# Attention core in plain fp32 with head pairs on two column tiles, and VectorE's share of the depthwise convolution summed in a PSUM bank

## The chip, the cores and the metric

The kernel is one program for one core of a Trainium2 chip. The metric is the device time of one execution in microseconds; several executions are taken and their median is given. The profile is of one further execution.

The engines are named as in the profile: PE is TensorE (matrix products; PEld its weight loads), DVE VectorE, ACT ScalarE, POOL GpSimd, SP SyncE, which issues the transfers. [...]

## The reference

A first block of two layers works on 512 tokens of 1024 channels; then a second block (a recurrent token mixer and a layer of experts) follows, which the change doesn't touch. Each layer of the first block is a mixer, a cross attention to 256 memory tokens and a feed-forward net. The mixer is what the change is about:

```python
def mla_group(c_q, c_kv, k_r, cos, sin, q_norm_g, w_uq, kv_norm_g, w_ukv):
    q = (rms_norm(c_q, q_norm_g) @ w_uq).reshape(B, S, MLA_HEADS, QK_NOPE_DIM + QK_ROPE_DIM)   # 8 heads, 64 + 32
    q_nope, q_rope = q[..., :QK_NOPE_DIM], apply_rope(q[..., QK_NOPE_DIM:], ...)
    kv = (rms_norm(c_kv, kv_norm_g) @ w_ukv).reshape(B, S, MLA_HEADS, QK_NOPE_DIM + V_HEAD_DIM)
    k_nope, v = kv[..., :QK_NOPE_DIM], kv[..., QK_NOPE_DIM:]
    k_rope = apply_rope(k_r, cos, sin)
    for start in range(0, S, Q_BLOCK):                      # 4 blocks of 128 queries
        end = start + Q_BLOCK
        s = einsum(q_nope[:, start:end], k_nope[:, :end]) + einsum(q_rope[:, start:end], k_rope[:, :end])
        s = where(mask, s * scale, -inf)                    # causal in chunks of 64
        p = softmax(s)
        outs.append(einsum('bhqk,bkhd->bqhd', p, v[:, :end]))

def conformer_conv_group(u, dw_w, dw_b, norm_g, norm_b):    # 512 channels, 31 taps
    a, g = split(u, 2)
    h = a * sigmoid(g)
    h = causal depthwise convolution of h with dw_w, + dw_b
    return silu(layer_norm(h, norm_g, norm_b))

def hybrid_mixer(x, ...):
    proj = x @ w_in + b_in                                  # c_q 256, c_kv 256, k_r 32, u 1024 columns
    return concatenate([mla_group(c_q, c_kv, k_r, ...), conformer_conv_group(u, ...)]) @ w_o
```

## The kernel before

The program is written with named tile pools, and a scheduler sets the order on each engine from a simulated timeline; the code gives data flow, tile pools and program order. The order of the built program is therefore shown below where it matters.

Most products are made at nearly fp32 accuracy from fp32r operands: each operand is kept as a high part and the remainder, and `mm3` (L155 to L159) issues three matmuls. `weight` (L134) loads a block of weights into a tile `wr`, ScalarE copies the high part (L148), and VectorE or GpSimd subtracts (L152); every `pool_lo`-th block goes to GpSimd. `split_ps` (L126) does the same from a PSUM bank: ScalarE copies the high part (L128), VectorE subtracts it (L130). `rstd` (L179) puts a power -1/2 on GpSimd (L185). A `ring` hands out the eight PSUM banks `q0` to `q7` in turn; `cm` is a pool of two 128 x 512 tiles.

`mixer` (L438) runs per layer. `latent(c)` projects the tokens onto 256 (c_q) or 288 columns (c_kv and k_r), squares and sums on ScalarE (L467), scales on VectorE (L469) and transposes. `gated(i)` projects two channel blocks of 128 (a block lies on the partitions, the 512 tokens along the row), applies the sigmoid (L487) and multiplies (L488); `conv_start` (L658) writes tap 30 and the bias into `acc`. The four blocks are the convolution's channels 0 to 3. The order in the code is latent(0), gated(0), latent(1), the keys' rotary part (L498 to L504, copied to four key tiles), the queries, gated(2), the keys' and values' weights, the values.

The attention goes through the heads. Two heads' keys come from `keys` (every second head; L573 copies the upper 64 rows down), the transposed query from `query`. For each of four blocks of queries: scores (one `mm3` on at least 256 keys), the row's maximum on VectorE (L604), the exponential with its sum on ScalarE (L607), the reciprocal on VectorE (L609), the scaling on ScalarE (L610), transposes on TensorE (L163), `split_ps` of the transposed probabilities. Then the output of a head: `mm3` with 128 columns of values, of which the head's own 64 are kept, and a `split_ps` of 64 rows. The code of the convolution, `conv` (L660), stands behind the heads, and the scheduler brings it forward into the gaps. VectorE has channel 0 and three quarters of channel 2, one operation a tap, with the running sum `acc` in SBUF (L669). GpSimd has channels 1 and 3 and the last quarter of channel 2: a product into a `cm` tile, by ScalarE (L673) for taps 10 to 29 of channel 1, by GpSimd itself (L675) otherwise, and an addition (L676). Behind it come the normalization over the channels (L638 to L647) and the output projection (`out_proj`).

## Time and profile before

| | us |
|---|---|
| median of 3 runs | 2641.08 |
| lowest and highest | 2638.80, 2645.98 |
| profiled execution | 2640.32 |
| its span, first to last instruction | 2638.1 |

| engine | busy us | share of the span |
|---|---|---|
| PE | 2460.6 | 93% |
| DVE | 1412.5 | 54% |
| ACT | 915.9 | 35% |
| POOL | 745.8 | 28% |

The mean granted clock of TensorE is 0.958 of full speed. The share of busy time is a mean over stages with different limits: for a change in the mixer the rows of the mixer's own stretch are to be read, which is about 37 to 260 us in layer 0 and 866 to 1090 us in layer 1. [...]

### The profile page before, as it was taken

The page shows a single profiled execution, that of the slowest core. Times are in us where ns is not written, and L with a number is a line of the kernel's source. Part 1 is how long each engine was busy: PE and PEld are TensorE (multiplying, and loading weights), DVE is VectorE, ACT ScalarE, POOL GpSimd, SP SyncE. Part 2 cuts the span into 40 slices and gives each one's busy share as a digit, 9 for nine tenths or more (in the row PEclk, how much of TensorE's full clock was granted, in tenths as well). Part 3 has the DMA queues.
Part 4 walks back from the last instruction along what each step waited for, and adds up shares of the span by engine and source line. Part 5 has one row for each costly group of instructions (what it writes and reads, how often), then busy time and mean ns, then how long its engine had stood idle before and what let it go on. Part 6 is the DMA issues. An engine that isn't in the chain of part 4 may idle for free.

```text
span 2638.1 us, 33264 instructions
## 1 busy us (share of the span) xinstructions
PE 2460.6 (93%) x12892; PEld 1858.1 (70%) x12892; DVE 1412.5 (54%) x2235; ACT 915.9 (35%) x1659; POOL 745.8 (28%) x627
## 2 busy tenths in 40 slices
...
GB/s 152 75 15 64 168 80 80 152 165 139 160 160 139 76 49 41 72 152 89 73 105 104 80 65 96 81 41 96 17 33 53 188 215 409 409 409 409 409 409 262
DMA packets 207513, 395.16 MB, mean 150 GB/s; under 512 B 24080, under 2 KB 115352, under 8 KB 207356
## 3 DMA queue, kind: packets, MB, share of 16 engines
...
q8 instruction: 101, 1.65, 0.3%
q14 instruction: 56, 0.46, 0.1%
...
## 4 chain that ended last, share of the span: by engine, by line
PE 76%; DVE 16%; ACT 3%; issue 2%; DMA 1%; POOL 1%; SPq 0%; DVEq 0%; POOLq 0%; ACTq 0%
PE q L157 17%; PE q L158 16%; PE q L159 16%; PE q L1756 12%; DVE t L669 4%; PE q L163 4%; PE q L1793 2%; DVE wl L152 1%; PE q L1731 1%; PE q L1183 1%; PE q L1188 1%; PE q L1757 1%; DVE t L130 1%; DVE xt L281 1%; DVE s L1159 1%
## 5 line engine op out<-in xcount | busy, mean ns | idle before, releaser
L157 PE MATMUL q<-t,wh 128*128 128x512 f32 (+1 forms) x1320 | 493.3, 375 | 16.1 <-DVE t L130 6.1
L159 PE MATMUL q<-t,wl 128*128 128x512 f32 (+1 forms) x1320 | 490.8, 374 | 8.8 <-DVE wl L152 5.6
L158 PE MATMUL q<-t,wh 128*128 128x512 f32 (+1 forms) x1320 | 492.8, 374 | 2.0 <-DVE t L1484 1.1
L148 ACT ACTIVATE wh<-wr 128x1024 fp32r<-128x1024 f32 (+4 forms) x280 | 289.0, 1034 | 491.7 <-PE q L159 213.2
L152 DVE TENSOR_TENSOR wl<-wr,wh 128x1024 fp32r<-128x1024 f32 (+2 forms) x206 | 266.3, 1296 | 207.8 <-ACT wh L148 203.3
L157 PE MATMUL q<-wh,t 128*128 128x512 f32 (+4 forms) x964 | 364.7, 383 | 8.9 <-ACT wh L148 3.7
L158 PE MATMUL q<-wl,t 128*128 128x512 f32 (+4 forms) x964 | 364.5, 379 | 4.5 <-DVE wl L538 2.2
L159 PE MATMUL q<-wh,t 128*128 128x512 f32 (+4 forms) x964 | 360.8, 379 | 0.6 <-DVE t L130 0.4
L152 POOL TENSOR_TENSOR wl<-wr,wh 128x1024 fp32r<-128x1024 f32 (+3 forms) x74 | 186.7, 2525 | 597.4 <-ACT wh L148 539.1
L157 PEld LDWEIGHTS q<-t,wh 128*128 128x128 f32 x1320 | 251.3, 191 | 66.2 <-DVE t L130 7.2
L159 PEld LDWEIGHTS q<-t,wl 128*128 128x128 f32 x1320 | 251.7, 191 | 51.4 <-DVE wl L152 6.9
L158 PEld LDWEIGHTS q<-t,wh 128*128 128x128 f32 x1320 | 251.6, 191 | 44.2 <-DVE t L1484 1.4
L185 POOL TENSOR_TENSOR sm<-sm,mhalf 128x1 f32<-128x1 f32 (+3 forms) x75 | 73.6, 983 | 738.4 <-DVE sm L183 736.9
L157 PEld LDWEIGHTS q<-wh,t 128*128 128x128 f32 x964 | 184.5, 192 | 50.3 <-DVE xt L292 6.4
L158 PEld LDWEIGHTS q<-wl,t 128*128 128x128 f32 x964 | 184.8, 192 | 38.3 <-DVE wl L538 2.7
L159 PEld LDWEIGHTS q<-wh,t 128*128 128x128 f32 x964 | 184.3, 192 | 35.3 <-issue 0.9
L676 POOL TENSOR_TENSOR t<-t,cm 128x128 f32<-128x128 f32 (+10 forms) x180 | 196.3, 1091 | 26.0 <-ACT cm L673 19.1
L803 POOL TENSOR_TENSOR t<-cm,t 128x512 fp32r<-128x512 f32 x44 | 70.5, 1603 | 302.6 <-ACT t L802 302.6
L163 PE MATMUL q<-ident,s 128*128 128x128 f32 (+3 forms) x538 | 98.1, 292 | 54.5 <-DVE s L1694 13.2
L128 ACT ACTIVATE t<-q 128x512 fp32r<-128x512 f32 (+1 forms) x172 | 89.4, 543 | 144.4 <-PE q L163 100.5
L163 PEld LDWEIGHTS q<-ident,s 128*128 128x128 f32 (+3 forms) x538 | 65.5, 147 | 100.7 <-issue 26.9
L130 DVE TENSOR_TENSOR t<-q,t 128x512 fp32r<-128x512 f32 (+1 forms) x172 | 103.6, 620 | 56.2 <-ACT t L128 55.8
...
## 6 DMA issues: line engine op xcount, KB each, us to landing
...
```

The lines of the kernel that those rows point to most:

```text
L128: nc.scalar.activation(hi, ps, AF.Copy, scale=1.0 if scale is None else scale)
L130: nc.vector.tensor_tensor(out=lo, in0=ps, in1=hi.bitcast(F32), op=OP.subtract)
L148: nc.scalar.activation(hi, raw, AF.Copy)
L152: e.tensor_tensor(out=lo, in0=raw, in1=hi.bitcast(F32), op=OP.subtract)
L157: m(out, ah, bh, start=first, stop=False)
L158: m(out, ah, bl, start=False, stop=False)
L159: m(out, al, bh, start=False, stop=last)
L163: self.nc.tensor.transpose(out, in_, self.ident[:n, :n])
L185: nc.gpsimd.tensor_tensor(out=r, in0=v, in1=self.mhalf[:, :n], op=OP.pow)
L669: e.scalar_tensor_tensor(a, h, w, a, op0=OP.mult, op1=OP.add)
L676: e.tensor_tensor(out=a, in0=a, in1=m, op=OP.add)
L1756: mm(ps[lo_, :], x, raw[:, c0], start=first, stop=last)
```

## The change

The queries, the keys, the values and the transposed probabilities are kept once, in fp32, and multiplied in plain fp32. The scores are one matmul on the valid keys only. The outputs are made for two heads at a time: each head's 64 columns of values go to one of two column tiles of TensorE and to the lower or upper 64 partitions of one bank, and one `split_ps` of 128 rows serves both. What was a `split_ps` ahead of it becomes one copy: the keys' lower half on VectorE (L571 of the new file) and upper half on ScalarE (L572), the query and the values on ScalarE (L581, L549), the transposed probabilities on VectorE (L609). Two key tiles instead of four hold two heads each, and the rotary part goes into them by two copies (L506, L507) in place of a split and three copies.

In the convolution VectorE has channels 0 and 2 whole: a product with the bias added (L662), 30 operations whose running sum is read from and written to PSUM bank 7 (L666; the last one writes `acc`), and a copy of the first 30 columns (L667). GpSimd has channels 1 and 3; ScalarE makes the products of taps 8 to 29 of channel 1 and 14 to 29 of channel 3. `gated(2)` stands right behind `gated(0)`, ahead of `latent(1)`; `pool_lo` becomes 5 ahead of `latent(1)`; the rings are cut so that bank 7 stays free.

```diff
@@ -455,7 +455,7 @@
         ck = self.t8([2, 2, 512])
         def latent(c):
             c0, n = (0, 256) if c == 0 else (256, 288)
-            ring = self.ring(*range(4 * c, 4 * c + 4))
+            ring = self.ring(0, 1, 2, 3)
             ps = self.tok_cols(w_in, c0, n, xT, ring, tokens_first=c == 0)
             ss = self.sm([NT])
             for t in range(NT):
@@ -479,7 +479,7 @@
         acc = self.t8([4, 512], F32)
 
         def gated(i):
-            ring = self.ring(0, 1, 2, 3)
+            ring = self.ring(4, 5, 6, 3)
             pa_ = self.fm_pair(w_in, 544 + i * 128, xT, ring)
             pg = self.fm_pair(w_in, 1056 + i * 128, xT, ring)
             for j in range(2):
@@ -487,24 +487,27 @@
                 nc.scalar.activation(sg, pg[j], AF.Sigmoid, bias=cv[:, i + j, 35:36])
                 nc.vector.scalar_tensor_tensor(hs[:, i + j, :], pa_[j], cv[:, i + j, 34:35], sg,
                                                op0=OP.add, op1=OP.mult)
-                self.conv_start(hs, acc, cv, i + j)
+                if i + j in self.CONV_POOL:
+                    self.conv_start(hs, acc, cv, i + j)
 
         latent(0)
         gated(0)
+        gated(2)
+        self.pool_lo = 5
         latent(1)
         kr = krt.rearrange("p t (h d) -> p t h d", h=1)
         self.rope(kr[:, :, :, 64:80], kr[:, :, :, 80:96], 0, NT, 1)
 
-        ps = self.ring(4)()
+        ps = self.ring(6)()
         for t in range(NT):
             self.tr(ps[:100, t * 128:(t + 1) * 128], krt[:, t, :])
-        kts = [self.n4([2, 512], F32R) for _ in range(4)]
-        self.split_ps(ps[64:100, :], kts[0][64:100, 0, :], kts[0][64:100, 1, :])
-        for k in kts[1:]:
-            nc.vector.tensor_copy(k[64:100], kts[0][64:100])
-        ring = self.ring(4, 5, 6, 7)
+        kts = [self.n4([2, 512]) for _ in range(2)]
+        tail = ps[64:100, None, :].to_broadcast([36, 2, 512])
+        nc.scalar.activation(kts[0][64:100], tail, AF.Copy)
+        nc.vector.tensor_copy(kts[1][64:100], tail)
+        ring = self.ring(4, 5, 6)
         qt = [self.t8([2, 8, 100], F32) for _ in range(2)]
         for i in range(2):
             nc.scalar.activation(qt[i][:, :, :, 96:100],
@@ -521,11 +524,8 @@
                                      ps.rearrange("p (h d) -> p h d", h=4), AF.Copy, scale=QSCALE)
         for i in range(2):
             self.rope(qt[i][:, :, :, 64:80], qt[i][:, :, :, 80:96], 2 * i, 2, 8)
-        gated(2)
-        self.stage(f"win_c{l}")
-        self.pool_lo = 5
         self.stage(f"win_u{l}")
-        ring = self.ring(4, 5, 6, 7)
+        ring = self.ring(0, 1, 2, 3)
         w_ukv = A["mla_w_ukv"][l].rearrange("(k p) (h d) -> p k h d", p=128, h=8)
 
         def kv_weight(d0):
@@ -540,39 +540,36 @@
 
         wkh, wkl = kv_weight(0)
         wvh, wvl = kv_weight(64)
-        vh, vl = self.t8([NT, 512]), self.t8([NT, 512])
+        vt = self.t8([NT, 512], F32)
         for t in range(NT):
             ps = ring()
             s = slice(t * 128, (t + 1) * 128)
             for k in range(2):
                 self.mm3(ps, ck[:, 0, k, s], ck[:, 1, k, s], wvh[:, k, :], wvl[:, k, :], k == 0, k == 1)
-            self.split_ps(ps, vh[:, t, :], vl[:, t, :])
+            nc.scalar.activation(vt[:, t, :], ps, AF.Copy)
 
         self.stage(f"qv{l}")
         yT = FM(self, 8, 512)
-        sring, tring, cring = self.ring(0, 1), self.ring(2, 3, 4, 5), self.ring(6, 7)
-        ptas = [[self.s2([2, 256], F32R) for _ in range(2)] for _ in range(2)]
-        ptbs = [self.t8([2, 4, 256]) for _ in range(2)]
+        sring, tring, cring = self.ring(0, 1), self.ring(2, 3, 4), self.ring(5, 6)
+        mm = nc.tensor.matmul
+        ptas = [[self.s2([2, 256]) for _ in range(2)] for _ in range(2)]
+        ptbs = [self.t8([2, 4, 256], F32) for _ in range(2)]
         for i in range(2):
             for j in range(2):
-                nc.gpsimd.tensor_copy(ptas[i][j][:, 1, 0:128], self.zeros.to_broadcast([128, 128]))
-                nc.gpsimd.tensor_copy(ptbs[i][:, j, 3, 0:128], self.zeros.to_broadcast([128, 128]))
+                nc.gpsimd.memset(ptas[i][j][:, 1, 0:128], 0.0)
+                nc.gpsimd.memset(ptbs[i][:, j, 3, 0:128], 0.0)
+        def key(h):
+            return kts[h % 4 // 2][:, h % 2, :]
 
         def keys(h):
             ps = cring()
             for k in range(2):
                 s = slice(h * 64, h * 64 + 128)
                 self.mm3(ps, wkh[:, k, s], wkl[:, k, s], ck[:, 0, k, :], ck[:, 1, k, :], k == 0, k == 1)
-            for i in range(2):
-                kk = kts[(h + i) % 4]
-                if i == 0:
-                    src = ps[0:64, :]
-                else:
-                    tmp = self.s2([512])
-                    nc.scalar.activation(tmp[0:64, :], ps[64:128, :], AF.Copy)
-                    src = tmp[0:64, :]
-                self.split_ps(src, kk[0:64, 0, :], kk[0:64, 1, :])
+            nc.vector.tensor_copy(key(h)[0:64], ps[0:64, :])
+            nc.scalar.activation(key(h + 1)[0:64], ps[64:128, :], AF.Copy)
 
         qs = {}
 
@@ -580,9 +577,9 @@
             ps = tring()
             for t in range(NT):
                 self.tr(ps[:100, t * 128:(t + 1) * 128], qt[t // 2][:, t % 2, h, :])
-            qh, ql = self.s2([512], F32R), self.s2([512], F32R)
-            self.split_ps(ps[:100, :], qh[:100, :], ql[:100, :])
-            qs[h] = qh, ql
+            q = self.s2([512])
+            nc.scalar.activation(q[:100, :], ps[:100, :], AF.Copy)
+            qs[h] = q
 
         keys(0)
         query(0)
@@ -591,15 +588,13 @@
                 if h % 2 == 1:
                     keys(h + 1)
                 query(h + 1)
-            kh, kl = kts[h % 4][:, 0, :], kts[h % 4][:, 1, :]
-            qh, ql = qs.pop(h)
-            ptb = ptbs[h % 2]
-            halves = (ptas[h % 2], (ptb[:, 0], ptb[:, 1]))
+            kh, q = key(h), qs.pop(h)
+            pair = h // 2 % 2
+            pts = [(ptas[pair][i], ptbs[pair][:, i]) for i in range(2)]
             for t in range(NT):
-                n, nv = max(256, (t + 1) * 128), (t + 1) * 128
-                s = slice(t * 128, (t + 1) * 128)
+                nv = (t + 1) * 128
                 ps = sring()
-                self.mm3(ps[:, :n], qh[:100, s], ql[:100, s], kh[:100, :n], kl[:100, :n], True, True)
+                mm(ps[:, :nv], q[:100, t * 128:nv], kh[:100, :nv], start=True, stop=True)
                 nm = self.sm([1])
                 nc.vector.tensor_reduce(nm, ps[:, :nv], axis=AX.X, op=OP.max, negate=True)
                 p = self.s2([512])
@@ -611,18 +606,18 @@
                 pt = tring().rearrange("p (k t) -> p k t", k=4)
                 for k in range(t + 1):
                     self.tr(pt[:, k, :], p[:, k * 128:(k + 1) * 128])
-                dh, dl = halves[t // 2]
-                s = slice((t % 2) * 128, (t % 2) * 128 + 128)
-                self.split_ps(pt[:, :t + 1, :], dh[:, :t + 1, s], dl[:, :t + 1, s])
-            ps = cring()
-            hp = slice((h // 2) * 128, (h // 2) * 128 + 128)
-            for i in range(2):
-                dh, dl = halves[i]
-                s = slice(i * 256, (i + 1) * 256)
-                for k in range(2 * i + 2):
-                    self.mm3(ps[:, s], vh[:, k, hp], vl[:, k, hp], dh[:, k, :], dl[:, k, :], k == 0, k == 2 * i + 1)
-            hs_ = slice((h % 2) * 64, (h % 2) * 64 + 64)
-            self.split_ps(ps[hs_, :], yT.hi(h // 2)[hs_, :], yT.lo(h // 2)[hs_, :])
+                nc.vector.tensor_copy(pts[h % 2][t // 2][:, :t + 1, (t % 2) * 128:(t % 2) * 128 + 128], pt[:, :t + 1, :])
+            if h % 2:
+                ps = cring()
+                for i in range(2):
+                    n = 2 * i + 2
+                    for k in range(n):
+                        for j in range(2):
+                            hd = slice((h - 1 + j) * 64, (h + j) * 64)
+                            mm(ps[j * 64:j * 64 + 64, i * 256:(i + 1) * 256], vt[:, k, hd], pts[j][i][:, k, :],
+                               start=k == 0, stop=k == n - 1)
+                self.split_ps(ps, yT.hi(h // 2), yT.lo(h // 2))
         self.conv(hs, acc, cv)
 
         self.stage(f"attn{l}")
@@ -648,10 +643,9 @@
         return yT
 
 
-    CONV_DVE = (((0, 0, 512),), ((2, 0, 384),))
-    CONV_POOL = (((1, 0, 512),), ((3, 0, 512),), ((2, 384, 512),))
-    conv_act = [(1, j) for j in range(10, TAPS)]
+    CONV_DVE = (0, 2)
+    CONV_POOL = (1, 3)
+    conv_act = [(1, j) for j in range(8, TAPS)] + [(3, j) for j in range(14, TAPS)]
 
     def conv_start(self, hs, acc, cv, i):
 
@@ -659,27 +653,27 @@
 
     def conv(self, hs, acc, cv):
 
         nc = self.nc
-        def tap(e, i, t0, t1, j):
-            h, a, w, d = hs[:, i, :], acc[:, i, :], cv[:, i, j:j + 1], 30 - j
-            a0 = max(t0, d)
-            a, h = a[:, a0:t1], h[:, a0 - d:t1 - d]
-            if e is nc.vector:
-                e.scalar_tensor_tensor(a, h, w, a, op0=OP.mult, op1=OP.add)
-            else:
-                m = self.cm()[:, :t1 - a0]
+        ring = self.ring(7)
+        for i in self.CONV_DVE:
+            sums = ring()
+            w = lambda j: cv[:, i, j:j + 1]
+            nc.vector.tensor_scalar(sums, hs[:, i, :], w(30), w(31), op0=OP.mult, op1=OP.add)
+            for j in range(29, -1, -1):
+                d = 30 - j
+                out = sums[:, d:] if j else acc[:, i, d:]
+                nc.vector.scalar_tensor_tensor(out, hs[:, i, :512 - d], w(j), sums[:, d:], op0=OP.mult, op1=OP.add)
+            nc.vector.tensor_copy(acc[:, i, :30], sums[:, :30])
+        for i in self.CONV_POOL:
+            for j in range(29, -1, -1):
+                d = 30 - j
+                m = self.cm()[:, :512 - d]
                 if (i, j) in self.conv_act:
-                    nc.scalar.activation(m, h, AF.Copy, scale=w)
+                    nc.scalar.activation(m, hs[:, i, :512 - d], AF.Copy, scale=cv[:, i, j:j + 1])
                 else:
-                    e.tensor_scalar(m, h, w, 1.0, op0=OP.mult, op1=OP.mult)
-                e.tensor_tensor(out=a, in0=a, in1=m, op=OP.add)
-        for e, groups in ((nc.vector, self.CONV_DVE), (nc.gpsimd, self.CONV_POOL)):
-            for pieces in groups:
-                for j in range(29, -1, -1):
-                    for i, t0, t1 in pieces:
-                        tap(e, i, t0, t1, j)
+                    nc.gpsimd.tensor_scalar(m, hs[:, i, :512 - d], cv[:, i, j:j + 1], 1.0, op0=OP.mult, op1=OP.mult)
+                nc.gpsimd.tensor_tensor(out=acc[:, i, d:], in0=acc[:, i, d:], in1=m, op=OP.add)
 
     def memory_keys(self, l):
 
```

New line numbers of the attention: scores L597, maximum L599, exponential L602, reciprocal L604, scaling L605, copy of the probabilities L609, outputs L618.

VectorE, layer 0, about the first maximum of the attention (before L604, now L599); `t_202` is the gated input, `t_203` is `acc`. Before:

```order
L130 TENSOR_TENSOR s_1015<-q_1009,s_1014 100x512
L669 SCALAR_TENSOR_TENSOR t_203<-t_202,cvec,t_203 128x378
L130 TENSOR_TENSOR n_690<-s_1005,n_690 64x512
L130 TENSOR_TENSOR s_1024<-q_1018,s_1023 100x512
L669 SCALAR_TENSOR_TENSOR t_203<-t_202,cvec,t_203 128x377
L604 TENSOR_REDUCE sm<-q_1027 128x1
L130 TENSOR_TENSOR n_691<-q_1118,n_691 64x512
L669 SCALAR_TENSOR_TENSOR t_203<-t_202,cvec,t_203 128x376
L609 RECIPROCAL sm<-sm 128x1
L604 TENSOR_REDUCE sm<-q_1043 128x1
L669 SCALAR_TENSOR_TENSOR t_203<-t_202,cvec,t_203 128x375
```

Now, with `q_1633` for the sums of channel 2 in bank 7:

```order
L666 SCALAR_TENSOR_TENSOR q_1633<-t_202,cvec,q_1633 128x484
L666 SCALAR_TENSOR_TENSOR q_1633<-t_202,cvec,q_1633 128x483
L666 SCALAR_TENSOR_TENSOR t_203<-t_202,cvec,q_1633 128x482
L667 COPY t_203<-q_1633 128x30
L599 TENSOR_REDUCE sm<-q_1007 128x1
L604 RECIPROCAL sm<-sm 128x1
L599 TENSOR_REDUCE sm<-q_1020 128x1
L609 COPY s_970<-q_1017 128x128
L604 RECIPROCAL sm<-sm 128x1
L599 TENSOR_REDUCE sm<-q_1034 128x1
L571 COPY n_819<-q_1219 64x512
```

Before, part of the convolution stands between the operations of the first heads; now all 62 of its operations stand ahead of the first maximum, and the heads follow without it.

ScalarE, layer 0, about the first exponential (before L607, now L602). Before:

```order
L128 ACTIVATE s_1014<-q_1009 100x512
L128 ACTIVATE n_690<-s_1005 64x512
L128 ACTIVATE s_1023<-q_1018 100x512
L128 ACTIVATE n_691<-q_1118 64x512
L607 ACT_TABLE_LOAD
L607 ACTIVATE s_1033,sm<-q_1027,sm 128x128
L610 ACTIVATE s_1033<-s_1033,sm 128x128
L607 ACTIVATE s_1049,sm<-q_1043,sm 128x256
L128 ACTIVATE s_982<-q_1039 128x128
L610 ACTIVATE s_1049<-s_1049,sm 128x256
L607 ACTIVATE s_1066,sm<-q_1060,sm 128x384
```

Now, with `cm` for products that GpSimd adds:

```order
L673 ACTIVATE cm<-t_202,cvec 128x500
L581 ACTIVATE s_998<-q_993 100x512
L581 ACTIVATE s_1005<-q_1000 100x512
L673 ACTIVATE cm<-t_202,cvec 128x499
L602 ACT_TABLE_LOAD
L602 ACTIVATE s_1011,sm<-q_1007,sm 128x128
L673 ACTIVATE cm<-t_202,cvec 128x498
L605 ACTIVATE s_1011<-s_1011,sm 128x128
L602 ACTIVATE s_1024,sm<-q_1020,sm 128x256
L673 ACTIVATE cm<-t_202,cvec 128x497
L605 ACTIVATE s_1024<-s_1024,sm 128x256
```

Before, no product of the convolution is left here; now 13 of channel 3's 16 products stand ahead of the first exponential and three between the first operations of head 0.

## Rows read from the trace of the kernel before

**Rows 1.** The head of the page.
```profile
span 2638.1 us, 33264 instructions
```

**Rows 2.** Chain of waits, 20 to 260 us, shares of that stretch by line.
```profile
by line: DVE t L669 21.0%; PE q L157 10.0%; PE q L158 9.7%; PE q L159 9.3%; issue 7.4%; DVE wl L152 4.5%; PE q L163 3.4%; DVE t L130 3.2%; DVE n L130 2.8%; ACT s L607 2.7%; ACT s L610 2.6%; ACT t L128 2.0%; DVE s L130 1.7%; DVE s L469 1.7%;
```

**Rows 3.** Windows: us, busy us (records) of PE, PEld, DVE, ACT, POOL; clock.
```profile
120.00:140.00 20.00, 12.06 (x41) 8.75 (x40) 19.93 (x25) 8.50 (x14) 19.77 (x22) 0.77 0.37 111
140.00:160.00 20.00, 15.90 (x55) 12.48 (x55) 19.87 (x38) 11.10 (x27) 19.84 (x16) 0.50 0.00 0
```

**Rows 4.** Two longer windows of layer 0, columns as in rows 3.
```profile
58.60:143.50 84.90, 67.83 (x317) 56.27 (x315) 83.36 (x101) 43.37 (x73) 70.96 (x55) 0.88 0.27 75
183.00:231.00 48.00, 42.97 (x257) 35.76 (x258) 33.21 (x81) 37.54 (x94) 40.71 (x66) 0.96 0.18 56
```

**Rows 5.** Line L669 alone in windows: VectorE's busy us (operations), clock, DMA.
```profile
58.60:143.50 84.90, 44.37 (x37) 0.88 0.27 75
143.50:231.00 87.50, 20.43 (x24) 0.84 0.10 31
183.00:231.00 48.00, 0.00 (x0) 0.96 0.18 56
```

**Rows 6.** Timeline of VectorE: start, us, line, tiles, count.
```profile
66.05 0.74 DVE L488 SCALAR_TENSOR_TENSOR t<-q,cvec,s 128x512 f32<-128x512 f32 x1
...
923.71 6.11 DVE L669 SCALAR_TENSOR_TENSOR t<-t,cvec,t 128x490 f32<-128x490 f32 x3
...
930.07 2.23 DVE L669 SCALAR_TENSOR_TENSOR t<-t,cvec,t 128x487 f32<-128x487 f32 x3
```

**Rows 7.** VectorE by line and form, 58.6 to 143.5 us: count, busy us, mean ns.
```profile
L152 DVE TENSOR_TENSOR wl<-wr,wh 128x1024 fp32r<-128x1024 f32 x5 | 6.5, 1298 | 0.0
...
L504 DVE CAST n<-n 36x1024 fp32r<-36x1024 f32 x3 | 3.5, 1225 | 0.0
```

**Rows 8.** Timeline of VectorE: first maximum, head outputs; layer 0, then layer 1.
```profile
143.46 0.27 DVE L604 TENSOR_REDUCE sm<-q 128x1 f32<-128x128 f32 x1
...
182.74 0.67 DVE L130 TENSOR_TENSOR t<-q,t 64x512 fp32r<-64x512 f32 x1
...
231.03 0.69 DVE L130 TENSOR_TENSOR t<-q,t 64x512 fp32r<-64x512 f32 x1 [0.36 <-ACT t L128]
...
973.62 0.27 DVE L604 TENSOR_REDUCE sm<-q 128x1 f32<-128x128 f32 x1
...
1058.22 0.69 DVE L130 TENSOR_TENSOR t<-q,t 64x512 fp32r<-64x512 f32 x1
```

**Rows 9.** Timeline of GpSimd: additions and products of the convolution.
```profile
94.87 6.23 POOL L676 TENSOR_TENSOR t<-t,cm 128x502 f32<-128x502 f32 x4
...
1011.60 1.35 POOL L675 TENSOR_SCALAR cm<-t,cvec 128x495 f32<-128x495 f32 x2
1012.93 2.38 POOL L676 TENSOR_TENSOR t<-t,cm 128x495 f32<-128x495 f32 x2
```

**Rows 10.** ScalarE by line and form, 183 to 231 us.
```profile
L128 ACT ACTIVATE t<-q 128x512 fp32r<-128x512 f32 x5 | 2.9, 585 | 3.3 <-PE q L163 3.2
```

**Rows 11.** Timeline of TensorE: fp32r at both clocks, then fp32 on column tiles.
```profile
128.40 0.39 PE L159 MATMUL q<-wh,t 128*128 128x512 f32 x1
128.63 0.40 PE L157 MATMUL q<-wh,t 128*128 128x512 f32 x1
...
140.16 0.63 PE L157 MATMUL q<-t,wh 128*128 128x512 f32 x1
140.59 0.63 PE L158 MATMUL q<-t,wh 128*128 128x512 f32 x1
...
2203.28 0.59 PE L1756 MATMUL q<-wr,t 128*64 128x512 f32 x1
...
2203.71 0.59 PE L1756 MATMUL q<-wr,t 128*64 128x512 f32 x1
```

**Rows 12.** Timeline of TensorE at the end of layer 1's mixer.
```profile
1084.79 0.47 PE L163 MATMUL q<-ident,s 128*128 128x128 f32 x1 [4.75 <-DVE s L638]
```

## The prediction

> **What bounds the kernel now.** I read the page's head first, then the chain of waits over the mixer of layer 0, then a table by windows. Over the whole program TensorE is busy nearly all the time, and the slices behind a mixer are full, so only the two mixers (37 to 260 us, and 866 to 1090 us) can move. The head gives a span of 2638.1 us [rows 1]. The profiled execution took 2640.32 us, 0.76 under the median of 2641.08; I subtract from 2640.3 and call the result a median.
>
> In the mixer of layer 0 the longest single item on the chain is the convolution's VectorE line L669, with 21% [rows 2]. [...] From the first maximum at 143.46 to the last output half at 231.03, eight heads take 87.6 us [rows 8]. Head 2 ends at 182.74 [rows 8], so the first three took 39.3 us (13.1 each) and the last five 48.3 (9.7 each). In the last five no L669 runs [rows 5], and TensorE has 43.0, ScalarE 37.5, VectorE 33.2 and GpSimd 40.7 busy of 48 [rows 4]. Layer 1 is alike: its last half starts at 1058.22 [rows 8].
>
> **The change: the VectorE convolution.** 60 L669 a layer become 62 operations (two products, 60 sums) plus two copies of 30 columns. Before, 37 stand ahead of the first maximum and take 44.4 us, a mean of 1.20; the other 24 records take 20.4, inside the first three heads [rows 5]. Undisturbed, three in a row took 2.23, 0.74 a step; six microseconds earlier three of the same took 6.11, 2.04 each [rows 6]. What stretches it shows in one pair: L488, same instruction but with an operand in PSUM, took 0.74 at 66.05 [rows 6]; L669 has both operands in SBUF, and GpSimd is working at the time. The new sum reads one operand from PSUM, so I price it like L488: 62 x 0.74 = 45.9 us. No row here shows VectorE writing a running sum in PSUM, so the bounds are 0.74, since no row of this width is shorter, and 1.5, if the write costs as much again. I take the row of L488 because it shares instruction, width and source.
>
> All 62 now stand ahead of the first maximum in VectorE's queue. VectorE is busy 83.4 us from 58.60 to 143.50 [rows 4], 39.0 of it on other work. Of that go three casts of L504 (3.5 us) [rows 7] and about six subtractions of 0.67 for keys, query and values (4 us); about one L152 at 1.30 [rows 7] comes over from GpSimd. So 45.9 + 32.8 = 78.7 us instead of 83.4. Against this, the gated block's second half now goes ahead of the second latent half: that latent's square sums wait on ScalarE behind 22 products (before 20), its reciprocal roots on GpSimd behind 22 additions, and VectorE's next operations wait for those roots. I give this 0 to 10 us and take 6. The first maximum then comes at 58.6 + 78.7 + 6 = 143: **no gain there.**
>
> **GpSimd and ScalarE.** GpSimd loses the 128-wide quarter of channel 2 (30 products and 30 additions) and 18 products; it keeps 60 additions and 22 products. An addition takes 2.38/2 = 1.19 us undisturbed and 6.23/4 = 1.56 beside L669; a product 1.35/2 = 0.68 [rows 9]. From about 68 us: 60 x 1.19 to 1.56, 22 x 0.68, and some 12 for weights and roots, ends at 166 to 189, before the attention does. ScalarE's products are paced by GpSimd through two buffers, and 13 of the second channel's 16 stand ahead of the first exponential: 43 additions and 8 products must be done. 68 + 43 x 1.3 + 5.4 + 5 = 134, so behind VectorE's 143 they cost nothing; were that cover gone, they would set the start. In layer 1 the old tail disappears: there the last additions hold TensorE until 1084.79, where it had idled 4.75 us [rows 12]; with the transposes ahead of it and some matmuls at the lower clock I count 6.
>
> **The heads.** On TensorE, 512 columns of fp32r take 0.23 us at the upper level (128.40 to 128.63) and 0.43 at the lower (140.16 to 140.59) [rows 11]. Plain fp32 on two 64-column tiles is in the experts' line L1756: 0.43 from record to record, two records to a matmul, so 0.86 for 512 columns of both tiles [rows 11]. Scores: 3 x 1408 columns at 0.23/512 = 1.90 become 1280 at 0.86/512 = 2.15. Output: 3 x 1536 columns = 2.07 become half of 1536 at 0.86/512, 1.29. TensorE saves 0.5 us a head, 4 a layer: hardly the point. ScalarE does 37.5/5 = 7.5 a head now [rows 4]. It loses the high copy of the transposed probabilities, four a head of at most 0.58 [rows 10], about 1.7, and some 0.9 of key and output copies: 4.9. VectorE does 6.6 and loses about 1.3. A head bound by ScalarE in today's proportion would take 9.7 x 4.9/7.5 = 6.3; one with no gain 9.7; TensorE's own work is about 5.7 at the upper level. I take 7.0, near the lower end because all engines but GpSimd have less to do and three hand-overs (the lows of query, keys and probabilities) vanish. TensorE works with gaps before the first maximum, so it starts at the lower level as today [rows 3]; I add 3 us. The end comes at 143 + 3 + 8 x 7 = 202 instead of 231: 29 us. In today's last heads TensorE also fits in some matrix work of the output projection, 9 products of three by 0.23 more than the new order has: minus 6 at most, hidden in part, I take 2. That is **27 in layer 0**. Layer 1's loop is 84.6 us long today (973.62 to 1058.22 [rows 8]); 3 + 56 in its place, less the 2, plus 6 from the tail: **30**. Sum 57: **2583 us**, 2.2% faster.
>
> [...] L488 at 66.05 and the three L669 at 930.07 last the same, 0.74 each [rows 6]. [...]
>
> **Rivals.** (a) *GpSimd paces the start.* Its additions stay at 1.56: the first exponential comes at 68 + 67 + 10 = 145, VectorE waits on the roots until 150, heads take 7.5: end 150 + 3 + 60 = 213, gain 16 and 19, **2605**. For: GpSimd is as full as VectorE in 120 to 160 [rows 3]. Against: what disturbed it is largely gone. (b) *The stretch stays* although one operand lies in PSUM: 62 x 1.20 = 74, 28.5 more a layer, which is all of the gain: **2640**, no change. Against: L488 [rows 6]. (c) *Slower: the sum in PSUM is dear.* Place: VectorE's queue ahead of the first maximum, where before 24 of 60 operations lay behind it. At 1.4 the start is 143 + 62 x 0.66 = 184, the end 243, 41 later than forecast in each layer: 2583 + 82 = **2665**. It decides from 57/124 = 0.46 more a step, 1.20. For: no row writes PSUM there and each operation reads what the one ahead wrote. Against: L669 in SBUF has the same dependence at 0.74. (d) *Everything at its cheap end:* no wait for roots, fewer stretched operations, start 131, heads 6.3: end 131 + 3 + 50 = 184, gain 45 and 48, **2547**.
>
> **How the numbers follow.** Forecast 0.55, (a) 0.16, (b) 0.06, (c) 0.10, (d) 0.13. The likeliest gives 2583. The range goes from 2540, just under (d), to 2622, which is (a) with a head of 8.5 (16 us more); below lies 0.04, above 0.16, (b) and (c). 0.3%, about 8 us, is what can be told from no change here. Faster: forecast, (a) and (d), 0.84; same: (b), 0.06; slower: (c), 0.10.
>
> **What would show it.** In the profile after: sums on VectorE at about 0.74 with no long ones beside GpSimd; the first maximum at 140 to 147; ScalarE's exponentials not idle for GpSimd; heads of 7 us; the last probability handled at about 200 and 1030; no TensorE idle time for GpSimd near the end of layer 1's mixer. I am wrong if the sums take over 1.1 us, if the first maximum comes past 160, or if TensorE stays at the lower level over most of the heads, where 5.7 us of work become 10.6.

## The result and the profile after

The changed kernel takes 2605.68 us (median of 4 runs, 2600.66 to 2608.54) against 2643.18 us for the kernel before in the same sessions: a ratio of 0.9858, with a 95% interval from 0.9833 to 0.9882. That is 1.4% faster, where the forecast was 2583 us, 2.2%; it lies inside the range. The span of the profiled execution fell from 2638.1 [rows 1] to 2598.4 us, by 39.7. The total is nearly the 2605 of rival (a); what happened is not what (a) describes, as the part on the prediction shows.

A sum on VectorE cost what was forecast. The line L666 by itself (`q` is a PSUM bank, `t` and `cvec` lie in SBUF; columns: engine, operation, tiles, count, then shortest, median and longest duration in ns, first and last start):

```profile
L666 DVE SCALAR_TENSOR_TENSOR q<-t,cvec,q x116: 711/735/756, 55.0 to 947.6; 128x511 f32<-128x511 f32 x4, 128x510 f32<-128x510 f32 x4, 128x509 f32<-128x509 f32 x4, 128x508 f32<-128x508 f32 x4
```

A sum takes 0.735 us in the median and never over 0.756, where three of the sums in SBUF took 2.04 us each in [rows 6]. On the timeline of VectorE, the first maximum and the last output half of the two layers (as in [rows 8]):

```profile
137.78 0.28 DVE L599 TENSOR_REDUCE sm<-q 128x1 f32<-128x128 f32 x1
...
203.82 0.67 DVE L130 TENSOR_TENSOR t<-q,t 128x512 fp32r<-128x512 f32 x1
...
949.10 0.28 DVE L599 TENSOR_REDUCE sm<-q 128x1 f32<-128x128 f32 x1
...
1012.62 0.67 DVE L130 TENSOR_TENSOR t<-q,t 128x512 fp32r<-128x512 f32 x1
```

The first maximum comes at 137.78 (143.46 before), the last output half at 203.82 (231.03 before). The windows that answer [rows 3] and [rows 4] (columns as there; the last is the stretch of the heads):

```profile
120.00:140.00 20.00, 7.64 (x20) 4.58 (x20) 18.44 (x24) 9.74 (x17) 11.77 (x11) 0.61 0.17 53
140.00:160.00 20.00, 19.61 (x86) 11.48 (x84) 12.03 (x34) 15.35 (x38) 18.34 (x19) 0.79 0.09 27
...
137.80:192.40 54.60, 50.12 (x239) 28.15 (x239) 33.11 (x99) 42.63 (x108) 30.06 (x32) 0.90 0.16 49
```

From 140 to 160 TensorE now does 19.6 of 20 us at a clock of 0.79, where it did 15.9 at 0.50. From 120 to 140 it does only 7.6, since the work ahead of the first maximum is not through. VectorE is full there, but only 4.3 us of its work from 120 to 137.78 are sums; 11.6 are the rotary part of the queries (L261 to L266). TensorE's longest wait, 9.31 us at 128.62, is for ScalarE's copy of the keys (L572), which itself waits for VectorE's copy (L571; 4.20 us of ScalarE's time ahead of 127.97).

To see where time went, each kernel's trace can be laid beside that of before at places that the change does not touch. In the list below an anchor is the start of the same instruction in both; the number is after minus before, in us of the trace.

| anchor (its start before) | after minus before |
|---|---|
| layer 0: last output half of the heads (231.0) | -27.2 |
| layer 0: end of the output projection, its last product (272.4) | -26.4 |
| start of layer 1's mixer (first L488, 885.8) | -20.1 |
| layer 1: last output half (1058.2) | -45.6 |
| layer 1: end of the output projection, its last product (1106.9) | -52.2 |
| behind layer 1's cross attention (1283) | -46.5 |
| second block, token mixer (1866) | -47.5 |
| second block, behind it (2038) | -40.8 |
| end (2627) | -39.6 |

At the ends of the two output projections 26.4 and 32.1 us are gained, 58.5 together; the forecast was 27 and 30. Of these, 6.3 and 5.7 are given back right behind each projection (from 310 us to the next mixer the trace stays 20 us ahead), and 6.7 in the second block, whose code the change does not touch.

**Behind the projection.** TensorE's timeline of the changed kernel, from the last product of layer 0's projection to the first of the memory keys, and then the same place before:

```profile
246.19 1.36 PE L163 MATMUL q<-ident,t 128*128 128x128 f32 x11
247.39 1.47 PE L163 MATMUL q<-ident,xt 128*128 128x128 f32 x12
248.62 0.37 PE L157 MATMUL q<-t,wh 128*128 128x256 f32 x1
250.00 0.65 PE L163 MATMUL q<-ident,xt 128*128 128x128 f32 x4 [1.01 <-DVE xt L294]
252.93 0.39 PE L157 MATMUL q<-t,wh 128*128 128x256 f32 x1 [2.28 <-DVE t L130]
```

```profile
272.59 0.60 PE L163 MATMUL q<-ident,t 128*128 128x128 f32 x4
272.94 0.36 PE L157 MATMUL q<-t,wh 128*128 128x256 f32 x1
```

Before, the transposes of the memory tokens (`ident,t`) were all but four done earlier, and the keys started 0.35 us behind the last four. After, eleven of the sixteen stand behind the projection's last product, VectorE is full with the layer's normalization (9.9 of 10 us from 240 to 250), and the keys wait for low parts that VectorE subtracts: 2.28 us at 252.93. Ahead of that the transposes of the mixer's tokens (`ident,xt`) wait 1.01 us for VectorE at 250.00. From 250 to 260 the granted clock is 0.83.

**In the second block.** One instruction ahead of the loss and one behind it, in before and after:

```profile
1865.90 0.43 DVE L1383 COPY n<-t 128x512 f32<-128x512 f32 x1 [2.46 <-ACT t L1536]
...
2038.03 0.67 DVE L1577 TENSOR_REDUCE sm<-s 128x4 f32<-128x512 f32 x1
```

```profile
1818.36 0.43 DVE L1377 COPY n<-t 128x512 f32<-128x512 f32 x1 [2.46 <-ACT t L1530]
...
1997.18 0.67 DVE L1571 TENSOR_REDUCE sm<-s 128x4 f32<-128x512 f32 x1
```

172.1 us have become 178.8. TensorE's windows there, first after, then before:

```profile
1902.00:1912.00 10.00, 8.23 (x59) 6.75 (x60) 8.62 (x29) 6.78 (x22) 4.33 (x3) 0.88 0.17 54
1912.00:1922.00 10.00, 8.54 (x40) 7.39 (x38) 5.76 (x16) 6.99 (x19) 2.54 (x2) 0.50 0.00 1
1922.00:1932.00 10.00, 9.97 (x68) 9.53 (x67) 6.18 (x14) 6.91 (x17) 2.54 (x2) 0.77 0.26 79
```

```profile
1950.00:1960.00 10.00, 8.13 (x72) 6.37 (x71) 7.70 (x26) 9.69 (x30) 5.18 (x4) 1.00 0.00 1
1960.00:1970.00 10.00, 9.99 (x63) 9.51 (x62) 7.99 (x17) 8.23 (x20) 2.74 (x2) 0.66 0.26 80
1970.00:1980.00 10.00, 10.00 (x93) 10.00 (x92) 7.59 (x18) 7.81 (x20) 0.00 (x0) 1.00 0.00 1
```

The clock is granted at 0.50 or 1.00 in both traces: of the changed kernel's windows of 2 us from 100 to 240 us, 55 read 1.00, 12 read 0.50, and three hold a change from one to the other. After, a stretch at 0.50 follows some 10 us in which TensorE worked with gaps (8.2 of 10 us); before, where it had done 8.1 of 10 us, the dip is to 0.66 and shorter. The order differs here between the two kernels: by the traces of this stretch, 34 of VectorE's 249 operations, 23 of ScalarE's 215 and 200 of TensorE's 1300 stand elsewhere, although their code is the same. The scheduler sets the whole program's order from one simulated timeline; presumably that timeline reaches this place with other transfers and buffers free, which no run shows.

### The profile page after: what moved, and what is told of

It is laid out like the page before. It is cut to its first block, busy times and chain, and to the rows that moved or that the text cites. A ratio compares the mean times of both kernels' runs of the same rounds, so it can differ in the third digit from the quotient of the medians.

```text
span 2598.4 us, 32699 instructions
## 1 busy us (share of the span) xinstructions
PE 2435.7 (94%) x12732; PEld 1809.2 (70%) x12732; DVE 1348.6 (52%) x2200; ACT 902.1 (35%) x1603; POOL 623.5 (24%) x468
## 4 chain that ended last, share of the span: by engine, by line
PE 79%; DVE 12%; ACT 3%; issue 2%; POOL 2%; DMA 1%; SPq 0%; DVEq 0%; POOLq 0%; ACTq 0%
PE q L157 17%; PE q L159 17%; PE q L158 17%; PE q L1750 12%; PE q L163 4%; PE q L1787 2%; DVE q L666 1%; PE q L1725 1%; PE q L1177 1%; DVE wl L152 1%; PE q L1751 1%; POOL t L676 1%; PE q L1182 1%; PE q L597 1%; DVE xt L281 1%
## 5 line engine op out<-in xcount | busy, mean ns | idle before, releaser
L148 ACT ACTIVATE wh<-wr 128x1024 fp32r<-128x1024 f32 (+3 forms) x280 | 289.1, 1034 | 517.9 <-PE q L159 228.1
L152 DVE TENSOR_TENSOR wl<-wr,wh 128x1024 fp32r<-128x1024 f32 (+4 forms) x209 | 270.1, 1294 | 218.1 <-ACT wh L148 211.4
L157 PE MATMUL q<-wh,t 128*128 128x512 f32 (+4 forms) x964 | 365.1, 383 | 11.4 <-ACT wh L148 4.2
L152 POOL TENSOR_TENSOR wl<-wr,wh 128x1024 fp32r<-128x1024 f32 (+2 forms) x71 | 178.5, 2515 | 618.3 <-ACT wh L148 547.7
L676 POOL TENSOR_TENSOR t<-t,cm 128x511 f32<-128x511 f32 (+14 forms) x120 | 151.5, 1263 | 30.8 <-ACT cm L673 25.0
L163 PE MATMUL q<-ident,s 128*128 128x128 f32 (+4 forms) x538 | 96.6, 289 | 43.9 <-DVE s L469 14.4
L163 PEld LDWEIGHTS q<-ident,s 128*128 128x128 f32 (+4 forms) x538 | 65.3, 145 | 102.0 <-issue 41.1
L128 ACT ACTIVATE t<-q 128x512 fp32r<-128x512 f32 (+1 forms) x124 | 63.4, 541 | 104.1 <-PE q L163 74.5
L1760 ACT ACTIVATE s<-q 128x512 f32<-128x512 f32 x16 | 9.6, 597 | 249.6 <-PE q L1751 249.6
```

The lines of the kernel that those rows point to most:

```text
L128: nc.scalar.activation(hi, ps, AF.Copy, scale=1.0 if scale is None else scale)
L148: nc.scalar.activation(hi, raw, AF.Copy)
L152: e.tensor_tensor(out=lo, in0=raw, in1=hi.bitcast(F32), op=OP.subtract)
L157: m(out, ah, bh, start=first, stop=False)
L163: self.nc.tensor.transpose(out, in_, self.ident[:n, :n])
L676: nc.gpsimd.tensor_tensor(out=acc[:, i, d:], in0=acc[:, i, d:], in1=m, op=OP.add)
```

## Experiments

Three questions were left: which part of the change brings the gain and how the parts need each other; whether the two losses have the causes named above; and what sets the pace of the heads.

### The two halves apart

`e_attn` takes the changed kernel's attention and leaves the convolution and the order of the gated halves as before. `e_conv` does the opposite.

> The attention half of the change alone: plain fp32, head pairs on two column tiles, single copies; the convolution, its split and the place of the second gated half as before. Theory (both halves are needed: the heads get cheaper, but the old convolution still stands between them on VectorE): L669 keep a mean over 0.9 us, the first maximum stays near 143, the first three heads stay slow and the last five go at about 8.2 instead of 9.7, so the attention ends 10 to 15 us earlier per layer; about 2620 us. Rival (the convolution hardly matters, the fp32 attention is the whole gain): as fast as the full change, about 2606 us.

> The convolution half of the change alone: sums in PSUM bank 7, channels 0 and 2 on VectorE, more products on ScalarE, the second gated half moved ahead; the attention in three fp32r products with high and low parts as before. Theory: sums at 0.74 us as in the changed kernel, first maximum near 139, heads at 9.7 us, so the attention ends near 217 instead of 231 and layer 1's idle tail goes; about 2622 us. Rival (the heads alone carry the gain): no faster than before, 2635 to 2645 us.

`e_attn` took 2641.48 us, a ratio of 1.0007 (0.9998 to 1.0017): no change. `e_conv` took 2629.31 us, 0.9957 (0.9942 to 0.9972). Together they give 0.9858, by the totals about four times the sum of its parts. But the totals also hold the second block, which neither half touches. At its start (1866 before) `e_attn` is 8.2 us ahead of before, `e_conv` 13.7 and the whole 47.5, over twice the sum of the parts. `e_attn` then loses 7.9 us in the second block:

```profile
1857.75 0.43 DVE L1377 COPY n<-t 128x512 f32<-128x512 f32 x1 [2.47 <-ACT t L1530]
...
2037.80 0.67 DVE L1571 TENSOR_REDUCE sm<-s 128x4 f32<-128x512 f32 x1
```

Its order there is the changed kernel's but for one operation of VectorE, so its total of nothing is a gain in the first block and the other order's loss behind it. Both expectations for `e_attn` were too fast even so, and its trace says why. TensorE's windows behind the heads, GpSimd's last additions of layer 0, and TensorE's wait for them in `e_attn`:

```profile
200.00:220.00 20.00, 18.47 (x101) 12.83 (x100) 12.04 (x28) 8.68 (x20) 11.55 (x26) 1.00 0.01 2
220.00:240.00 20.00, 10.39 (x51) 8.09 (x50) 7.97 (x14) 2.48 (x6) 14.81 (x36) 0.82 0.00 0
```

```profile
233.98 0.99 POOL L670 TENSOR_TENSOR t<-t,cm 128x128 f32<-128x128 f32 x2
...
235.02 0.69 PE L163 MATMUL q<-ident,t 128*128 128x128 f32 x2 [5.82 <-POOL t L670]
```

The heads end earlier (last output at 211.8), but GpSimd's additions go on to 235 and 1066, TensorE does 10.4 of 20 us from 220 to 240, and the memory keys start at 270.07 instead of 272.94. GpSimd's tail, which had been covered in layer 0, has become the bound: TensorE waits 5.82 us for it there. The changed kernel's GpSimd is through its additions at 170.9, since it has 60 a layer fewer operations of 128 columns and 18 products fewer. So the convolution's half removes what would otherwise hold the end, and the attention's half makes the heads short; each alone leaves the other in the way. `e_conv` keeps heads of about 10 us behind a first maximum at 140.08, as its expectation had it, and misses the expected total by 7 us: its layers gain 9.9 and 14.2 us to the ends of their projections, but 6.1 and 4.4 are given back right behind them and 3.0 in the second block.

### Does PSUM matter for the sum?

`e_sbuf` is the changed kernel with the sum in place in SBUF:

```diff
-            sums = ring()
+            sums = acc[:, i, :]
-                out = sums[:, d:] if j else acc[:, i, d:]
+                out = sums[:, d:]
-            nc.vector.tensor_copy(acc[:, i, :30], sums[:, :30])
```

> The changed kernel with VectorE's running sums in SBUF (in place in acc) instead of PSUM bank 7; the split over the engines and the queue order ahead of the first maximum as in the changed kernel. Its order in the second block is that of the kernel before, which by the runs so far is worth about 7 us against the changed kernel. Theory (an operand in PSUM keeps a sum from being stretched by GpSimd): the sums take 1.1 us or more in the mean instead of 0.74, with single ones over 2, GpSimd's additions get longer too, the first maximum comes 20 to 28 us later, near 160; about 2606 + 48 - 7 = 2645 us. Rival (the stretch came from the mix of work, not from the place of the sum): sums stay at 0.75 to 0.8, about 2600 us.

It took 2643.93 us, 1.0011 (1.0002 to 1.0020) of before: without PSUM the whole gain is gone. Its sums and GpSimd's additions, as groups of one line:

```profile
L665 DVE SCALAR_TENSOR_TENSOR t<-t,cvec,t x120: 705/1012/2790, 53.8 to 991.8; 128x511 f32<-128x511 f32 x4, 128x510 f32<-128x510 f32 x4, 128x509 f32<-128x509 f32 x4, 128x508 f32<-128x508 f32 x4
...
L674 POOL TENSOR_TENSOR t<-t,cm x120: 1035/1382/6410, 62.9 to 1033.2; 128x511 f32<-128x511 f32 x4, 128x510 f32<-128x510 f32 x4, 128x509 f32<-128x509 f32 x4, 128x508 f32<-128x508 f32 x4
```

Against 0.735 us in the median and 0.756 at most, a sum takes 1.012 and up to 2.790; GpSimd's additions go from 1.216 to 1.382 in the median, with single ones of up to 6.4 us. The mean of a sum is 1.15, as expected (1.1 or more). The first maximum comes at 159.51 instead of 137.78. So the sums and GpSimd's additions stretch each other when both operands of a sum lie in SBUF, and with one operand in PSUM the sums are not stretched: of the changed kernel's 120, 40 with an addition of GpSimd beside them from start to end took 0.712 to 0.752 us, 30 with none beside them 0.711 to 0.756. It is the operand read that counts, not the place written: the last sum of each channel reads PSUM and writes SBUF, and took 0.716 to 0.719 us in the changed kernel, all four times beside additions of GpSimd: nearly throughout at 84.96 and 896.72, for the last 0.3 us at 137.05 and 0.6 at 948.37. This decides rival (b) and rival (c) of the prediction: no stretch, and no price for a running sum in PSUM (0.735 us against 0.74 for an undisturbed L669).

The changed kernel still has such pairs. Two products of the queries' rotary part, alike in size and both with two operands in SBUF:

```profile
122.00 1.30 DVE L261 TENSOR_TENSOR s<-t,sin 128x256 f32<-128x256 f32 x1
...
127.86 0.41 DVE L263 TENSOR_TENSOR t<-t,cos 128x256 f32<-128x256 f32 x1
```

GpSimd adds from 118.17 to 125.6 and is idle from then to 129.31. And each of its ten additions over 1.7 us (up to 2.36) has beside it a weight subtraction of VectorE (L152 or L538), whose operands lie in SBUF.

### The losses behind the mixer

`e_mem` writes the memory tokens' transposes ahead of the projection, on banks 5 and 6:

```diff
+            mT = self.memory_tokens(l)          # the load and tr_tile of memory_keys, ring(5, 6)
             self.out_proj(A["mix_w_o"][l], yT, gb)
-            mT, kT = self.memory_keys(l)
+            mT, kT = self.memory_keys(l, mT)
```

> The changed kernel with the transposes of the memory tokens written ahead of the output projection instead of behind it, on other banks; nothing else. In the changed kernel they come behind the projection's last product, and TensorE idles some 6 us in each layer until their low parts are subtracted. Theory: this hand-over was hidden before, in gaps that the change closed; moved back under the projection it costs nothing, 6 us a layer: about 2594 us. Rival: the gap waits for something else there (the normalized tokens, weights), so the time stays near 2606 us.

2592.78 us, 0.9819 (0.9804 to 0.9834): 13 us less than the changed kernel by the medians, 10 by the two ratios, as expected. Its first block is 60.2 us ahead of before's instead of 46.5 (at 1283). In its trace the memory keys follow the projection at once:

```profile
248.14 0.82 PE L163 MATMUL q<-ident,xt 128*128 128x128 f32 x6
248.71 0.36 PE L157 MATMUL q<-t,wh 128*128 128x256 f32 x1
```

`e_best` adds one product on ScalarE, which makes the second block's order that of before:

```diff
-    conv_act = ... + [(3, j) for j in range(14, TAPS)]
+    conv_act = ... + [(3, j) for j in range(13, TAPS)]
```

> The kernel with the memory tokens' transposes ahead of the projection, and one product more on ScalarE (tap 13 of channel 3). By itself the extra product moves under a microsecond, but with it the order of the untouched second block comes out word for word as in the kernel before. Theory (the 7 to 8.5 us lost there come from the order): no loss in that stretch, about 2593 - 8 = 2585 us. Rival (the loss belongs to the faster first block, through transfers or the granted clock): about 2593 us.

2586.15 us, 0.9788 (0.9773 to 0.9804), 6.6 under `e_mem`, as expected. From 1866 to 2038 it loses 2.2 us against before, `e_mem` 8.5. `e_order` goes the other way: the kernel before, with one product more (tap 9 of channel 1), in the changed kernel's order.

> The kernel before with one product more on ScalarE (tap 9 of channel 1), which by itself moves under a microsecond on engines that don't end last there; with it the untouched second block comes out in the changed kernel's order on VectorE and ScalarE. Theory (the order costs the 7 us): the first block as before within 2 us, and 6 to 8.5 us lost between 1866 and 2038 us of the trace; about 2648 us. Rival (the loss is tied to the faster first block): about 2641 us.

2644.73 us, 1.0013 (1.0002 to 1.0025). The total moved by 4.9 us between the medians (3.4 by the ratio), less than the 7 expected; the first block came out 2.8 us shorter, where at most 2 were expected. The stretch itself shows the loss: the same two instructions as above, and the windows there.

```profile
1863.09 0.43 DVE L1383 COPY n<-t 128x512 f32<-128x512 f32 x1 [2.47 <-ACT t L1536]
...
2043.71 0.67 DVE L1577 TENSOR_REDUCE sm<-s 128x4 f32<-128x512 f32 x1
```

```profile
1946.00:1956.00 10.00, 8.68 (x64) 7.07 (x62) 9.28 (x33) 5.19 (x18) 3.54 (x3) 0.89 0.17 64
1956.00:1966.00 10.00, 8.49 (x47) 7.32 (x48) 5.94 (x18) 6.98 (x20) 3.33 (x3) 0.50 0.00 0
```

It is 180.6 us long instead of 172.1, with the same spell at 0.50, in a kernel whose first block is nearly as slow as before. In `e_s3` and `e_gated` (below), whose order there is that of before, it is 172.1 and 172.3 long, though their first blocks are 28 us slower and 60 us faster. All the traces together show three orders of this stretch. The order of before takes 172.1 to 174.3 us in seven kernels, the changed kernel's 178.8 to 180.7 in four (with `e_attn`, `e_mem` and `e_order`), and a third 175.1 to 175.4 in three (`e_conv`, `e_bmem`, `e_r1`). So the loss goes with the order and not with the faster first block. Which of the moved operations brings it was not tried, nor what the up to 2.2 us within the order of before are.

`e_bmem` moves the memory tokens' transposes in the kernel before.

> The kernel before with the transposes of the memory tokens written ahead of the output projection. Theory (before, they lay in gaps that the mixer's slow end left, so moving them gains nothing): the first block as before within 2 us; with the second block's order changed in part by the move, worth 0 to 4 us, 2641 to 2645 us. Rival (6 us a layer were lost there before, too): about 2630 us.

2651.06 us, 1.0046 (1.0030 to 1.0062). Nothing is gained there, as the theory has it, but the time is over both expectations: the first block is 4.1 us longer (at 1866), since the keys start at 279.24 instead of 272.94, and the second block 3.1, in the third order. Why the move costs that much in the first block is open.

### The place of the gated half

`e_gated` puts `gated(2)` and `pool_lo = 5` back behind the queries, all else as in the changed kernel.

> The changed kernel with the second gated half back behind the queries. Its order in the second block is that of the kernel before, so about 7 us must come back there: 2599 us if the place of the gated half is worth nothing. Theory (VectorE is full up to the first maximum whichever sums it has, so the place only changes where it waits): first maximum within 4 us of the changed kernel's 137.8 and 949.1, 2595 to 2607 us. Rival (channel 2's sums then come too late): first maximum past 150 and 960, over 2615 us.

2582.71 us, 0.9786 (0.9772 to 0.9799): 23 us faster than the changed kernel by the medians, 19 by the ratios and by the spans of the two traces, more than either side expected. In the traces 6.5 of it are the second block's order and 12.1 the first block: VectorE's timeline at the first maximum and the second channel's sums, and TensorE's windows.

```profile
105.24 0.81 DVE L662 TENSOR_SCALAR q<-t,cvec 128x512 f32<-128x512 f32 x1
...
121.17 0.29 DVE L599 TENSOR_REDUCE sm<-q 128x1 f32<-128x128 f32 x1 [0.37 <-PE q L597]
...
144.99 0.18 DVE L667 COPY t<-q 128x30 f32<-128x30 f32 x1
```

```profile
100.00:120.00 20.00, 16.90 (x77) 13.31 (x75) 18.86 (x22) 9.85 (x14) 18.43 (x24) 1.00 0.35 109
120.00:140.00 20.00, 15.16 (x45) 8.49 (x47) 17.23 (x39) 18.72 (x41) 15.54 (x14) 0.66 0.09 27
```

The first maximum comes at 121.17 instead of 137.78. The first L488 comes 2.3 us earlier (51.08), and from it to the first maximum VectorE has 65.9 us of work instead of 82.4: 19 of channel 2's sums, 14 us, whose input comes later, now lie between the operations of heads 0 to 2 instead of ahead of them. There they take the gaps in which VectorE waits for the other engines: the first three heads take 10.9, 11.4 and 8.8 us, but the last maximum still comes 9.4 us earlier. TensorE does 15.2 of 20 us from 120 to 140 instead of 7.6. So the place of the gated half, with `pool_lo`, cost the changed kernel 12 us of its first block.

### The pace of the heads

Three runs asked what sets it. I had put the pace at 8.2 by dividing the time from the first maximum to the last output half by eight; that counts the last head's end, 11.4 us with matrix products of the projection between, as pace. From the first query block of a head to that of the next, the changed kernel takes 50.5 us for seven heads in layer 0, 7.2 each, the first of them 9.5 at the lower clock (0.50), and the later ones 5.3 to 8.5, nearly all at the upper (0.99 in the mean).

> The changed kernel with a third PSUM bank for the scores (bank 7, free once the convolution is summed). Its order in the second block, which the change does not touch, comes out as in the kernel before, where the changed kernel's differs there. Theory: the head's pace of 8.2 us is set by hand-overs between the engines with only two score banks, so it falls to about 7.5, 5 us a layer; and the stretch of the second block in which the changed kernel lost 8 us against before is back at before's length because its order is: about 2588 us. Rivals: the pace stays at 8.2 (TensorE's own work is the limit); the 8 us stay lost, since they come from the granted clock by chance and not from the order: then 2598 to 2606 us.

`e_s3` took 2667.40 us, 1.0102 (1.0087 to 1.0117), and missed both ways of its expectation. Bank 7 was not free: the heads now share its ring with the sums, so the sums of both channels wait until the heads are nearly through. VectorE's timeline (first maximum, channel 0's first operation, last maximum, channel 2's first operation) and TensorE's windows of `e_s3`:

```profile
126.98 0.29 DVE L599 TENSOR_REDUCE sm<-q 128x1 f32<-128x128 f32 x1 [4.08 <-PE q L597]
...
179.90 0.81 DVE L662 TENSOR_SCALAR q<-t,cvec 128x512 f32<-128x512 f32 x1
...
181.21 0.68 DVE L599 TENSOR_REDUCE sm<-q 128x1 f32<-128x512 f32 x1
...
207.01 0.81 DVE L662 TENSOR_SCALAR q<-t,cvec 128x512 f32<-128x512 f32 x1
```

```profile
180.00:200.00 20.00, 10.48 (x55) 6.71 (x55) 18.92 (x30) 4.69 (x9) 0.00 (x0) 0.91 0.00 0
200.00:220.00 20.00, 1.51 (x6) 1.14 (x6) 19.08 (x28) 0.00 (x0) 0.00 (x0) 0.50 0.00 0
```

With the sums behind the heads TensorE does 1.5 of 20 us from 200 to 220. The heads themselves, from first to last maximum, take 54.2 us (126.98 to 181.21) against 54.6, at a clock of 0.99 instead of 0.90: a third bank shows no gain. The run also shows that VectorE's sums are not all that holds the first maximum: with none of them ahead of it, it comes only 10.8 us earlier than in the changed kernel, and later than in `e_gated`, which has 41 ahead of it. VectorE is busy 36 of the 73 us from the first L488 on, and the maximum waits 4.08 us for TensorE.

> The changed kernel without ScalarE's scaling of the probabilities by the reciprocal sum (left out, so the attention's output is not normalized). The heads take 8.2 us there, where I forecast 7.0. Theory (the chain of hand-overs inside a query block sets the pace, score to maximum to exponential to reciprocal to scale to transpose): taking one of its links away shortens the head by about 1 us or more, to about 7. Rival (TensorE's own work and its switches set the pace): 8.0 or more.

> The changed kernel with the scores made by one fp32r matmul (query and keys rounded to fp32r, so the scores are less exact) instead of plain fp32: 1280 columns a head at 0.23/512 instead of 0.86/512, 1.6 us less TensorE work a head. Theory (the hand-overs set the pace): some 0.3 to 0.8 us a head, since the score is a link of the chain too. Rival (TensorE's own work sets it): the head falls by the whole 1.6 us, to 6.6.

Each was executed once, with 2596.44 and 2606.49 us; `e_noscale` leaves out the scaling, and `e_r1` rounds the query and the keys. The stretch from first to last maximum, for the changed kernel (layer 1; layer 0 is shown above), then `e_noscale` and `e_r1`, layers 0 and 1 (length, busy us of TensorE, its weight loads, VectorE, ScalarE and GpSimd, clock):

```profile
949.10:1001.20 52.10, 47.51 (x238) 26.55 (x239) 32.04 (x98) 43.28 (x109) 32.42 (x34) 0.96 0.16 51
```

```profile
140.80:192.20 51.40, 46.80 (x240) 26.55 (x242) 33.76 (x100) 28.23 (x78) 29.78 (x32) 0.93 0.15 52
950.00:1001.80 51.80, 46.60 (x239) 26.46 (x241) 32.78 (x99) 27.85 (x78) 31.34 (x33) 0.93 0.15 52
```

```profile
140.90:198.50 57.60, 46.23 (x208) 27.08 (x209) 33.69 (x100) 42.67 (x108) 29.95 (x32) 0.79 0.14 46
954.90:1010.70 55.80, 44.13 (x209) 25.61 (x209) 31.92 (x97) 43.72 (x110) 32.47 (x34) 0.85 0.14 48
```

Without the scaling ScalarE does 28 us instead of 43, and the loop is 3.2 and 0.3 us shorter: that link is not what paces it. With some 1.6 us less TensorE work a head by the sum of the prediction, the loop is not shorter but 3.0 and 3.7 us longer, at a clock of 0.79 and 0.85 instead of 0.90 and 0.96. So neither expectation holds for the loop. TensorE worked with more gaps there (90.4 of 113.4 us busy, against 97.6 of 106.7) and was granted less clock. Where both had a clock of 1.00, in heads 3 to 5 of layer 1, `e_r1` is the faster one (first the changed kernel, then `e_r1`):

```profile
970.15:990.38 20.23, 19.09 (x104) 10.64 (x103) 12.76 (x41) 16.27 (x42) 14.76 (x17) 1.00 0.22 73
```

```profile
979.27:998.02 18.75, 14.74 (x86) 8.46 (x85) 11.46 (x38) 15.65 (x41) 10.36 (x12) 1.00 0.17 57
```

A head takes 6.25 us instead of 6.74, 0.5 less, as its theory has it, and not 1.6 less. What sets the 6.7 us of an undisturbed head is left open. TensorE is nearest to full, with 19.1 of 20.2 us, but its records outlast the distance to the next start (in the changed kernel two products of 512 columns, at 196.63 and 196.86, last 0.40 and 0.39 us and start 0.23 apart), so busy time is not work alone; and in `e_r1`, where it has 14.7 of 18.8 us, the head is only 0.5 us shorter.

### Put together

> The changed kernel with three things put together: the second gated half back behind the queries, the memory tokens' transposes ahead of the output projection, and two products more on ScalarE (tap 7 of channel 1, tap 13 of channel 3), with which the second block's order on ScalarE is that of the kernel before and on VectorE nearly so. Theory (the kernel with the gated half back still loses 6 us a layer between the projection and the memory keys): 2583 less 12, about 2571 us. Rival (the hand-over is covered by something else there, or the two products more delay the exponentials): 2580 us or more.

`e_final` took 2574.96 us, 0.9756 (0.9742 to 0.9769): faster than both kernels, by 31 us than the changed one between the medians and 27 by the ratios. It lies between the expected 2571 and the rival's 2580. Its first block is 70.4 us ahead of before's, 10.8 more than `e_gated`'s, and 1.9 are lost from 1866 to 2038.

## Why the prediction was right, and where it was short

- **The sums on VectorE.** Forecast 0.74 us a step, from L488 and the undisturbed L669; measured 0.735. The prediction's pair of rows shows less than was read in it: GpSimd was idle beside L488 at 66.05 (from 64.80 to 68.33), as it was beside the undisturbed L669 at 930.07, so this L488 could not show that an operand in PSUM keeps off the stretch. The other L488 of the kernel before do show it: four of the eight, at 124, 130, 954 and 958 us, ran beside GpSimd's work (products, casts and 0.3 us of an addition) and took 0.737 to 0.751; the four beside which it was idle took 0.744 to 0.753.

```profile
L488 DVE SCALAR_TENSOR_TENSOR t<-q,cvec,s x8: 737/748/753, 58.6 to 957.8; 128x512 f32<-128x512 f32 x8
```

- **The first maximum.** Forecast 143: 78.7 us of VectorE work and 6 of waiting, from 58.6. Measured 137.78. From the first L488, now at 53.37, it is 84.4 us against the forecast 84.7, but VectorE is busy 82.4 of them: 3.7 more than forecast, with 4 less of waiting, so the length came out by two errors that cancel. The rest of the 5.7 us gained is a start 5.2 us earlier, which no term of the sum has. Why it starts earlier is open. In layer 1 the start is no earlier than the trace is ahead anyway (20 us); there the length fell from 87.8 to 83.4. "No gain there" was nearly right, and `e_gated` shows that a part of the reason given, that all 62 operations stand ahead, is what the change lost.
- **GpSimd.** Forecast 166 to 189 for its end, measured 170.9; in layer 1 the tail is gone, as forecast (last addition done at 985, ahead of the last maximum at 1001).
- **The heads.** This term was too small. Forecast 3 + 56 = 59 us from the first maximum to the last output half; measured 66.0, and 63.5 in layer 1. The pace is as forecast, 50.5 us for the first seven heads with their slow start against 52. What is longer is the last head, 15.6 us to its output instead of 7, in which TensorE also does products of the projection. The end came at 203.82 instead of 202 only because the start was 5.2 us early: this is luck.
- **The sum.** Forecast 27 and 30 us; 26.4 and 32.1 at the ends of the projections. The terms are not those forecast: in layer 0 the first maximum gives 5.7 (forecast none), the heads 21.5 (29), and 0.8 is lost from there to the projection's end (2); in layer 1 the first maximum gives 4.4 (none), the heads 21.1 (26) and what lies behind them 6.6 (4, the tail of 6 less 2). So the agreement of the sums is in part luck. The step that failed outright is one that has no term: with "only the two mixers can move" the prediction took it that what is gained at the projection's end reaches the program's end. The hand-over to the memory keys took back 6.3 and 5.7, the second block 6.7, its last part 1.2, and 1.0 was gained between 1283 and 1866: 58.5 - 6.3 - 5.7 - 6.7 - 1.2 + 1.0 = 39.6, the difference of the spans (39.7) but for rounding.
- **Rivals.** (a) names 2605, which is what was measured, but its mechanism did not happen: GpSimd's additions took 1.216 us in the median instead of 1.56, and the first maximum came at 137.78, ahead of (a)'s first exponential at 145. Its loss lies in the mixers; the measured one lies behind them. (b) and (c) fell with the 0.735 us of a sum, and `e_sbuf` shows what (b) would have been. (d) did not happen either; a first maximum ahead of its 131 came only with another order, in `e_gated`, `e_final` (122.77) and `e_s3`.
